# RWKV-7 recurrence on one core: from 64-row and 64-column products per head to products on the whole TensorE array

## The chip, the cores and the metric

One core of a Trainium2 chip runs the whole program. The metric is the device time of one execution in microseconds (us), the median of several executions. Five engines work side by side, each through its own instructions in order: PE (TensorE, matrix products), DVE (VectorE), ACT (ScalarE), POOL (GpSimd) and SP, which here issues the DMAs.

## The reference, cut to what matters

The program is one step of a hybrid layer: 512 prompt frames and 32 sample frames, a combined input projection, three recurrences (Mamba-2 SSD, GLA, RWKV-7), output projections and a cross attention. The change touches the RWKV-7 branch, 16 heads of 64 x 64 state:

```python
def step(S, inp):
    r_t, w_t, k_t, v_t, kk_t, a_t = inp
    s_kk = jnp.einsum('bhvk,bhk->bhv', S, kk_t)
    S_new = (S * w_t[:, :, None, :] - s_kk[..., None] * (kk_t * a_t)[:, :, None, :]
             + v_t[..., None] * k_t[:, :, None, :]).astype(S.dtype)
    return S_new, jnp.einsum('bhvk,bhk->bhv', S_new, r_t)
...
o7, rwkv_new = _rwkv7_scan(r_h, hd(decay), k_h, v_h, kk, a_h, rwkv_h)
```

## The kernel before

**Tiling.** The frames are cut into chunks of 64: eight of the prompt (c = 0 to 7) and one of the sample (c = 8). Two heads share the 128 partitions (partitions 0 to 63 and 64 to 127), so there are eight pairs p of heads. Within a chunk the recurrence is written as matrix products with an inverse of a 64 x 64 triangular matrix; from chunk to chunk a state Sn is handed on. All products of the recurrence are plain float32; the profile records each of them as two MATMUL rows. The dense projections (tile pd, weights wh and wl, activations uh and ul) are split into high and low float32r parts, one row per product, 48 products for each of 158 blocks of 128 output columns.

**Threads per pair.** rw_A(p) (line 815) prepares the operands: AR (decayed keys in AR[.., 0, :], decayed queries in AR[.., 1, :]), PP (products of keys, tile pp), TK (values and keys by token, through DRAM). rw_I(p) (line 984) inverts: a DMA brings blocks of PP to tile nd, 31 pairs of POOL operations (im, td; lines 1011 and 1012) do the substitution, the result goes through DRAM into TT, is transposed on DVE (line 1022), and two sets of 32-row products (pW, pT) finish it. rw_C(p) (line 1043) is the recurrence, nine steps, c = 8 first. rw_N(p) normalises. The tiles AR, PP, TT, TK, GC of a pair stand in one of three slots.

**One step of rw_C** (lines 1063 to 1102) comes to PE three times, with other engines between:

- first visit (lines 1072 to 1077): keys times state, per head, to pa, and state times queries, per head, to po: four products of 64 x 64. DVE then forms R (line 1079).
- second visit (line 1083): the inverse TT times R, per head: two products of 64 x 64. ACT copies head 0 into TK and DVE head 1 (lines 1084, 1085).
- third visit (lines 1089 and 1092): the state update pS and the output po, per head, 128 rows by 64 columns: four products. DVE makes the new state Sn (line 1097), ACT copies the output into AR (line 1102).

At c = 0 there is no state yet, and the first visit is left out. So there are 64 first, 72 second and 72 third visits.

**Order.** A planner, class Sched (line 126), runs at build time. Every thread is a generator; the planner keeps estimated times for each engine, takes the ready thread of the highest priority and writes its instructions out. The dense products fill the time in which no thread of higher priority is ready, at most five between two looks (GRAIN = 5). mm() (line 226) holds the estimate of a product, with 90 and 105 ns for a change between float32r and float32. The result is a fixed order per engine; nothing is rearranged when it runs. The last 48 dense blocks of the projection (gates) have no one waiting for them until the end and serve as fill for the RWKV part and then for the GLA and SSD part.

Of the kernel before, what the change touches and what calls it, by code (L numbers as in the profile page):

```python
# [8 lines left out]
F32 = mybir.dt.float32  # L9
F32R = mybir.dt.float32r  # L10
I32 = mybir.dt.int32
# [114 lines left out]
class Sched:  # L126
# [99 lines left out]
    def mm(self, out, lhsT, rhs, start, stop, transpose=False, shared=False):  # L226

        n = rhs.free_size()
        k, m = lhsT.partition_size(), lhsT.free_size()
        if transpose:  # L230
            self.nc.tensor.transpose(out, lhsT, rhs)
            ns = 107.0
        else:
            self.nc.tensor.matmul(out, lhsT, rhs, start=start, stop=stop, skip_group_check=shared)  # L234
            if lhsT.dtype == F32R:
                ns = n / 2.4 + 12.7
            elif m <= 64:
                ns = max(60.0, n * 0.95 + 14)
            else:
                ns = max(210.0, n * 1.67)  # L240
        small = lhsT.dtype != F32R
        if self.small and not small:
            ns += 105
        elif small and not self.small:
            ns += 90
        self.small = small
        self.n_small = self.n_small + ns if small else 0.0
        if start:
            self.note("pe", ns, (out,), (lhsT, rhs))
        else:  # L250
            self.note("pe", ns, (), (lhsT, rhs))
            self.mark(out, 0, "pe", self.t["pe"])
# [72 lines left out]
def body(tc, I, O):  # L325
    nc = tc.nc
# [4 lines left out]
    def has(*names):  # L331
        return lambda: all(n in done for n in names)
# [12 lines left out]
    with tc.manual_schedule(), \  # L345
# [370 lines left out]
        EE = rwp.tile([128, 9, 65], F32, name="EE")  # L716

        def make_slot(pool, i):
            d = dict(AR=pool.tile([128, 9, 2, 64], F32, name=f"AR{i}"))
            d["PP"] = pool.tile([128, 9, 2, 2, 64], F32, name=f"PP{i}")  # L720
            d["TT"] = pool.tile([128, 9, 64], F32, name=f"TT{i}")
            d["TK"] = pool.tile([128, 2, 9, 2, 64], F32, name=f"TK{i}")
            d["GC"] = pool.tile([128, 9, 1], F32, name=f"GC{i}")
            return d
# [76 lines left out]
        def rows64(scr, h):  # L801

            return scr[:, h, 0:4096].rearrange("c (s t) -> s c t", t=64)
# [5 lines left out]
        def ch(a):  # L809
            return a.rearrange("p (c t) -> p c t", t=64)  # L810
# [4 lines left out]
        def rw_A(p):  # L815
# [3 lines left out]
            if p == 2:  # L819
                yield has("rwR")  # L820
            d = slot[p % NSLOT]
            w2h = rwp.tile([128, 2, 128], F32R, name="w2h", tag="w2h")
            yield S.stored(w2r)
            yield S.at(w2r)
# [68 lines left out]
            S.tt(ch(k7), ch(ks), tha, MUL, e="p")  # L893
            if p >= NSLOT:
                yield has(f"rwO{p - NSLOT}")
            ar = d["AR"]
            S.tt(ar[:, :, 0, :], ch(kk), EE[:, :, 0:64], MUL)
            yield S.free("v")
            S.stt(be, ch(kka), -0.5, Gi, MUL, MUL)
            S.cp(bk[64:128, :, 2, :], be[64:128])  # L900
            yield has(f"rs{p}")
            yield S.at(rs)
            S.tt(ar[:, :, 1, :], ch(rs), EE[:, :, 1:65], MUL)
            yield S.free("v")
            bee = sq
            gcol = d["GC"]
# [35 lines left out]
            for c0, cn in ((0, 4), (4, 4), (8, 1)):  # L942
                ps = []
                for _ in range(2):
                    ps.append((yield from bank("pp")))
                for c in range(cn):
                    for i in range(2):
                        hs = slice(64 * i, 64 * i + 64)
                        S.mm(ps[i][:, c * 128:c * 128 + 128], bk[hs, c0 + c, i:i + 2, :].rearrange("p a t -> p (a t)"),
                             ar[hs, c0 + c].rearrange("p a t -> p (a t)"), True, True)  # L950
                for i in range(2):
                    S.tt(pp[:, c0:c0 + cn, i].rearrange("p c a t -> p c (a t)"), ps[i][:, :cn * 128].rearrange("p (c x) -> p c x", c=cn),
                         C("m_rw").unsqueeze(1).to_broadcast([128, cn, 128]), MUL)
                yield S.free("v")
# [29 lines left out]
        def rw_I(p):  # L984
# [31 lines left out]
                S.store(out=blocks(d_scr)[:, g:32:3], in_=td[g * NB:g * NB + NB, 0:m])  # L1016
            yield S.stored(td)
            for h in range(2):
                S.dma(out=tt_[h * 64:h * 64 + 64], in_=rows64(d_scr, h))
            yield S.at(tt_)  # L1020
            x1 = rwr.tile([128, 8, 32], F32, name="x1", tag="itmp")
            nc.vector.transpose(x1, tt_[:, 0:8, 0:32])
            S.note("v", 340, (x1,), (tt_,))
            yield S.at(x1) + W["XM"]
            ps = yield from bank("pW")
            for c in range(8):
# [5 lines left out]
            ps = yield from bank("pT")  # L1032
            for c in range(8):
                for h in (0, 64):
                    S.mm(ps[h:h + 32, c * 32:c * 32 + 32], w[h + 32:h + 64, c, :], tt_[h + 32:h + 64, c, 32:64], True, True)
            for h in (0, 64):
                S.act(tt_[h:h + 32, 0:8, 32:64], ps[h:h + 32, :256].rearrange("p (c t) -> p c t", t=32), AF.Copy)
            done.add(f"rwI{p}")
            yield None

        IE = "pv"[W["IE"]]

        def rw_C(p):
# [12 lines left out]
            for c0, cn in ((4, 5), (0, 4)):  # L1056
                ps = yield from bank("pr")
                for c in range(cn):
                    for i in range(2):
                        hs, gs = slice(64 * i, 64 * i + 64), slice(64 - 64 * i, 128 - 64 * i)  # L1060
                        S.mm(ps[hs, c * 64:c * 64 + 64], PP[gs, c0 + c, i, 0, :], VU[gs, c0 + c, i, :], True, True)
                S.act(RV[:, c0:c0 + cn].rearrange("p c t -> p (c t)"), ps[:, :cn * 64], AF.Copy)
            for c in [8] + list(range(8)):
                Ss = s0r if c == 8 else (None if c == 0 else st_)
                pa = yield from bank("pc")
                pb = yield from bank("pc")
                pu = pa[:, 64:128], pb[:, 0:64]
                po, pS = pb[:, 64:128], pa[:, 128:192]
                if Ss is None:
                    R = RV[:, 0]  # L1070
                else:
                    for h in (0, 64):
                        hs = slice(h, h + 64)
                        S.mm(pa[hs, 0:64], AR[hs, c, 0, :], Ss[hs, :], True, True)
                    for h in (0, 64):
                        hs = slice(h, h + 64)
                        S.mm(po[hs], Ss[hs, :], AR[hs, c, 1, :], True, False, shared=True)
                    R = rwp.tile([128, 64], F32, name="R", tag="R", bufs=2)
                    S.tt(R, pa[:, 0:64], RV[:, c], ADD)
                yield S.at(R)  # L1080
                for i, h in enumerate((0, 64)):
                    hs = slice(h, h + 64)
                    S.mm(pu[i][hs], TTt[hs, c, :], R[hs, :], i == 0 or Ss is None, True, shared=i == 1)
                S.act(VU[0:64, c, 0, :], pu[0][0:64], AF.Copy)
                S.cp(VU[64:128, c, 1, :], pu[1][64:128])
                yield S.at(VU[0:64, c, 0, :], VU[64:128, c, 1, :]) + W["R2"]
                for i in range(2):
                    hs = slice(64 * i, 64 * i + 64)
                    S.mm(pS[hs], KB[:, c, i, :], VU[:, c, i, :], True, True)
                for i in range(2):  # L1090
                    hs = slice(64 * i, 64 * i + 64)
                    S.mm(po[hs], VU[:, c, i, :], PP[:, c, i, 1, :], Ss is None, True, shared=True)
                ns = rwp.tile([128, 64], F32, name="Sn", tag="S", bufs=2)
                if Ss is None:
                    S.cp(ns, pS)
                else:
                    S.stt(ns, Ss, GC[:, c, :], pS, MUL, ADD)
                if c >= 7:
                    S.store(out=O["rwkv_s" if c == 8 else "rwkv_p"][:, p], in_=ns)
                st_ = ns  # L1100
                yield S.at(ns)
                S.act(AR[:, c, 1, :], po, AF.Copy)
            done.add(f"rwC{p}")

        def rw_N(p):
# [2 lines left out]
            rwr = pools["rwR"][1]  # L1108
            d = slot[p % NSLOT]
            AR = d["AR"]  # L1110
            o7 = AR[:, :, 1, :]
            HC = ((0, 4, 0), (4, 4, 256), (8, 1, 512))

            def rows(t, c, n, o):
# [903 lines left out]
```

## Time and profile before

| what | us |
|---|---|
| median of three runs | 1344.29 (1342.06 to 1345.19) |
| the profiled execution | 1338.43 |
| its span, first to last instruction | 1336.6 |
| PE busy in the span | 1292.2 (97%) |
| DVE, ACT, POOL busy | 790.7, 633.8, 348.6 |

The span has four parts on PE: memory projections and the start (to about 190 us), the RWKV recurrence (194.5 to 630.5), GLA and SSD (about 710 to 932), and then gates, output projections and attention. Of a group of matrix products the busy time tells little, since records overlap: a record lasts some 290 ns while the next begins 125 ns later. What a product takes from PE is read as the distance from its start to the start of the next one.

### The profile page before, as it was taken

How to read it: one execution, taken by the hardware profiler on the slowest of the kernel's cores; microseconds unless marked ns; L12 is line 12 of the kernel's file. 1: busy time of each engine (PE TensorE's matmuls, PEld its weight loads, DVE VectorE, ACT ScalarE, POOL GpSimd, SP SyncE). 2: the span in 40 equal slices, each digit the busy share in tenths (PEclk: the TensorE clock that was granted, in tenths of full speed). 3: DMA queues.
4: the chain of work that ended last, by engine and by line, in shares of the span. 5: the costliest groups of instructions: out<-in, count | busy, mean ns of one | idle time of the engine just before them, and what ended most of it. 6: DMA issues, size and time to landing. Idle time of an engine off the chain costs nothing.

```text
span 1336.6 us, 28525 instructions
## 1 busy us (share of the span) xinstructions
PE 1292.2 (97%) x11416; PEld 1209.0 (90%) x11416; DVE 790.7 (59%) x1578; ACT 633.8 (47%) x1221; POOL 348.6 (26%) x712
## 2 busy tenths in 40 slices
PE   7899999999999999999899999999999999999997
PEld 6799998888888888898899989898999999989996
DVE  5747765756646574333546887863466756575543
ACT  4665455465655553353636355362545323544421
POOL 2701827356362724520112532420000000000000
PEclk9999999999999999999999999999999999999998
DMA  8443554445444354432421423432697446530301
GB/s 289 152 141 100 153 136 110 105 119 127 126 105 117 108 149 115 137 130 84 156 99 63 148 88 115 140 113 75 230 328 245 145 131 201 175 118 25 102 17 67
DMA packets 167557, 176.67 MB, mean 132 GB/s; under 512 B 99825, under 2 KB 122449, under 8 KB 167297
## 3 DMA queue, kind: packets, MB, share of 16 engines
q1 hardware_dynamic: 167280, 174.71, 42.9%
q8 instruction: 90, 1.47, 0.5%
q14 instruction: 43, 0.34, 0.1%
q10 hardware_dynamic: 144, 0.14, 0.0%
HBM read 134.01 MB, written 33.16 MB: 125 GB/s over the span
## 4 chain that ended last, share of the span: by engine, by line
PE 63%; DVE 4%; ACT 2%; DMA 2%; issue 1%; SPq 0%; DVEq 0%; ACTq 0%
PE pd L234 50%; PE pc L234 3%; PE py L234 1%; PE psc L234 1%; PE pO L234 1%; PE pov L234 1%; DMA wraw<-in_wall 1%; PE ph L234 1%; PE pp L234 1%; PE pss L234 1%; PE pS L234 1%; DVE wr L273 1%; DMA ab<-acs_d 1%; ACT L267 0%; PE pr L234 0%
## 5 line engine op out<-in xcount | busy, mean ns | idle before, releaser
L234 PE MATMUL pd<-uh,wl 128*128 128x272 f32 (+1 forms) x1632 | 483.9, 297 | 9.2 <-DVE wl L273 5.0
L234 PE MATMUL pd<-uh,wh 128*128 128x272 f32 (+1 forms) x1632 | 484.3, 297 | 0.0
L234 PE MATMUL pd<-ul,wh 128*128 128x272 f32 (+1 forms) x1632 | 476.6, 292 | 0.0
L234 PEld LDWEIGHTS pd<-uh,wl 128*128 128x128 f32 (+1 forms) x1632 | 307.4, 188 | 18.4 <-DVE wl L273 10.3
L234 PEld LDWEIGHTS pd<-uh,wh 128*128 128x128 f32 (+1 forms) x1632 | 307.7, 189 | 8.2 <-issue 2.4
L234 PEld LDWEIGHTS pd<-ul,wh 128*128 128x128 f32 (+1 forms) x1632 | 307.7, 189 | 4.2 <-issue 1.2
L273 DVE TENSOR_TENSOR wl<-wraw,wh 128x1024 fp32r<-128x1024 f32 x142 | 180.1, 1268 | 62.8 <-ACT wh L267 61.9
L267 ACT ACTIVATE wh<-wraw 128x1024 fp32r<-128x1024 f32 x142 | 149.6, 1054 | 66.0 <-PE pd L234 47.0
L234 PE MATMUL pd<-uh,wr 128*128 128x256 f32 (+1 forms) x768 | 152.6, 295 | 2.7 <-ACT uh L267 2.7
L234 PEld LDWEIGHTS pd<-uh,wr 128*128 128x128 f32 x768 | 122.4, 190 | 5.5 <-ACT uh L267 3.1
L273 POOL TENSOR_TENSOR macc<-macc,hrs 128x288 f32<-128x288 f32 x3 | 3.0, 1022 | 426.4 <-ACT hrs L267 426.4
L273 POOL TENSOR_TENSOR im<-td,nd 108x84 f32<-108x84 f32 (+23 forms) x248 | 89.1, 359 | 91.0 <-DMA nd<-n_scr 60.5
L234 PE MATMUL pd<-ul,wr 128*128 128x256 f32 (+1 forms) x384 | 111.3, 290 | 0.1
L273 POOL TENSOR_TENSOR td<-td,im 108x84 f32<-108x84 f32 (+23 forms) x248 | 99.2, 400 | 19.4
L234 PEld LDWEIGHTS pd<-ul,wr 128*128 128x128 f32 x384 | 73.0, 190 | 0.7 <-DVE ul L273 0.4
L267 ACT ACT_TABLE_LOAD x55 | 70.6, 1283 | 3.3 <-DVE tB L273 2.3
L278 DVE SCALAR_TENSOR_TENSOR fg<-fg,pd 128x272 f32<-128x272 f32 x48 | 20.6, 432 | 53.6 <-ACT fg L267 53.3
L267 ACT ACTIVATE TK<-pc 64x64 f32<-64x64 f32 x72 | 15.3, 213 | 72.0 <-PE pc L234 71.9
L267 ACT ACTIVATE lerpA<-pd,par 128x272 f32<-128x272 f32 x50 | 24.2, 485 | 44.2 <-PE pd L234 40.0
L234 PE MATMUL pd<-mnh,wh 128*128 128x256 f32 x128 | 37.0, 289 | 7.9 <-ACT mnh L267 6.7
L284 POOL TENSOR_SCALAR cs<-cs,par 128x544 f32<-128x544 f32 x8 | 8.3, 1043 | 139.3 <-DVE cs L273 51.5
L267 ACT ACTIVATE fg<-pd,dpar 128x272 f32<-128x272 f32 x48 | 23.2, 484 | 38.6 <-PE pd L234 30.8
(480 smaller groups left out, 2480.9 us busy)
## 6 DMA issues: line engine op xcount, KB each, us to landing
wraw<-in_wall SPq DMA_DIRECT2D x166, 512.0 KB
g_mg<-fg SPq DMA_DIRECT2D x24, 272.0 KB
mgt<-g_mg SPq DMA_DIRECT2D x24, 272.0 KB
TK<-tm SPq DMA_DIRECT2D x96, 64.0 KB
ab<-acs_d SPq DMA_DIRECT2D x8, 512.0 KB
nd<-n_scr SPq DMA_DIRECT2D x24, 144.0 KB
n_scr<-PP SPq DMA_DIRECT2D x16, 144.0 KB
TT<-d_scr SPq DMA_DIRECT2D x16, 144.0 KB
```

The costliest lines, as they stand in the source:

```text
L234: self.nc.tensor.matmul(out, lhsT, rhs, start=start, stop=stop, skip_group_check=shared)
L267: self.nc.scalar.activation(out=out, in_=in_, func=f, scale=scale, bias=bias)
L273: eng.tensor_tensor(out=out, in0=a, in1=b, op=op)
L278: self.nc.vector.scalar_tensor_tensor(out=out, in0=a, scalar=s, in1=b, op0=op0, op1=op1)
L284: eng.tensor_scalar(out=out, in0=a, scalar1=s1, scalar2=s2, op0=op0, **kw)
```

## The change

Both heads of a pair are now computed by one product on all 128 rows and columns, with the operands laid out as block diagonals:

- AR gets three parts: the keys of head 0 (zero in partitions 64 to 127), the keys of head 1 (zero in 0 to 63), the queries. TT becomes 128 wide, with the two inverses on its diagonal and zeros elsewhere. The zeros are written once per slot by four POOL memsets.
- First visit: one product (AR's two key parts, 128 x 128, with the state, 64 columns). The product of state and queries moves to the third visit.
- A new POOL operation per step forms Sd, the state as a block diagonal (128 x 128, state times a mask of ones).
- Second visit: one product of TT with R repeated twice (128 columns). One DVE copy_predicated with the mask takes both diagonal blocks into TK, in place of one copy on ACT and one on DVE.
- Third visit: three products of 128 x 128 with 128 columns: pS (both heads' keys with TK), po from Sd and the queries, po from TK and PP. Of pS and po only the diagonal blocks are used: DVE makes Sn, and ACT copies the output, in two halves of 64 partitions each.
- The transposes of TT on DVE are two of 64 partitions in place of one of 128.
- In the planner's estimate a "small" product is now one with under 128 rows or columns, whatever its type, and the change back costs 150.

```diff
-        small = lhsT.dtype != F32R
+        small = k < 128 or m < 128
         if self.small and not small:
-            ns += 105
+            ns += 150
...
-            d = dict(AR=pool.tile([128, 9, 2, 64], F32, name=f"AR{i}"))
+            d = dict(AR=pool.tile([128, 9, 3, 64], F32, name=f"AR{i}"))
-            d["TT"] = pool.tile([128, 9, 64], F32, name=f"TT{i}")
+            d["TT"] = pool.tile([128, 9, 128], F32, name=f"TT{i}")
...
+            if p < NSLOT:
+                for h in (0, 64):
+                    g = 64 - h
+                    for x in (d["AR"][h:h + 64, :, g // 64, :], d["TT"][h:h + 64, :, g:g + 64]):
+                        nc.gpsimd.memset(x, 0.0)
+                        S.note("p", 700, (x,), ())
...
-            S.tt(ar[:, :, 0, :], ch(kk), EE[:, :, 0:64], MUL)
-            yield S.free("v")
+            for i in range(2):
+                hs = slice(64 * i, 64 * i + 64)
+                S.tt(ar[hs, :, i, :], ch(kk)[hs], EE[hs, :, 0:64], MUL)
+                yield S.free("v")
...
-                S.dma(out=tt_[h * 64:h * 64 + 64], in_=rows64(d_scr, h))
+                S.dma(out=tt_[h * 64:h * 64 + 64, :, h * 64:h * 64 + 64], in_=rows64(d_scr, h))
...
-                    for h in (0, 64):
-                        hs = slice(h, h + 64)
-                        S.mm(pa[hs, 0:64], AR[hs, c, 0, :], Ss[hs, :], True, True)
-                    for h in (0, 64):
-                        hs = slice(h, h + 64)
-                        S.mm(po[hs], Ss[hs, :], AR[hs, c, 1, :], True, False, shared=True)
+                    S.mm(pa[:, 0:64], AR[:, c, 0:2, :].rearrange("p a t -> p (a t)"), Ss, True, True)
                     R = rwp.tile([128, 64], F32, name="R", tag="R", bufs=2)
                     S.tt(R, pa[:, 0:64], RV[:, c], ADD)
+                    Sd = rwp.tile([128, 2, 64], F32, name="Sd", tag="Sd", bufs=2)
+                    S.tt(Sd, both(Ss), two(C("blk1")), MUL, e="p")
                 yield S.at(R)
-                for i, h in enumerate((0, 64)):
-                    hs = slice(h, h + 64)
-                    S.mm(pu[i][hs], TTt[hs, c, :], R[hs, :], i == 0 or Ss is None, True, shared=i == 1)
-                S.act(VU[0:64, c, 0, :], pu[0][0:64], AF.Copy)
-                S.cp(VU[64:128, c, 1, :], pu[1][64:128])
-                yield S.at(VU[0:64, c, 0, :], VU[64:128, c, 1, :]) + W["R2"]
+                S.mm(pu, TTt[:, c, :], both(R), True, True)
+                nc.vector.copy_predicated(VU[:, c], two(C("blk1").bitcast(I32)), two(pu))
+                S.note("v", 203, (VU[:, c],), (pu,))
+                yield max(S.at(VU[:, c]), 0.0 if Ss is None else S.at(Sd))
+                S.mm(pS, KB[:, c].rearrange("p a t -> p (a t)"), VU[:, c], True, True)
+                if Ss is not None:
+                    S.mm(po, Sd.rearrange("p a t -> p (a t)"), both(AR[:, c, 2, :]), True, False)
+                S.mm(po, VU[:, c].rearrange("p a t -> p (a t)"), PP[:, c, :, 1, :], Ss is None, True)
+                ns = rwp.tile([128, 64], F32, name="Sn", tag="S", bufs=2)
                 for i in range(2):
                     hs = slice(64 * i, 64 * i + 64)
-                    S.mm(pS[hs], KB[:, c, i, :], VU[:, c, i, :], True, True)
-                for i in range(2):
-                    hs = slice(64 * i, 64 * i + 64)
-                    S.mm(po[hs], VU[:, c, i, :], PP[:, c, i, 1, :], Ss is None, True, shared=True)
...
+                    if Ss is None:
+                        S.cp(ns[hs], pS[hs, hs])
+                    else:
+                        S.stt(ns[hs], Ss[hs], GC[hs, c, :], pS[hs, hs], MUL, ADD)
...
-                S.act(AR[:, c, 1, :], po, AF.Copy)
+                for i in range(2):
+                    hs = slice(64 * i, 64 * i + 64)
+                    S.act(AR[hs, c, 2, :], po[hs, hs], AF.Copy)
```

What this makes of the order on each engine is seen in two places. The first is one step of the recurrence of the second pair (p = 1) on PE, before. In a row stand the tile written, the tiles read, and the rows and columns of the moving operand; "x2" is two in a row; numbers after a name tell tiles apart.

```order
L234 MATMUL pc<-Sn,AR_123 64x64 x2
L234 MATMUL pc<-AR_123,Sn 64x64 x2
L234 MATMUL pd<-uh,wh 128x272
...
L234 MATMUL pc<-R,TT_125 64x64 x2
L234 MATMUL pd<-uh,wl 128x272
...
L234 MATMUL pc<-TK_126 64x64 x2
L234 MATMUL pc<-PP_124,TK_126 64x64 x2
L234 MATMUL pn<-k_3509,blk_96 128x288 x4
```

The same pair's step in the changed kernel, on PE:

```order
L234 MATMUL pd<-uh,wl 128x272
L234 MATMUL pc<-Sn,AR_123 128x64
L234 MATMUL pp<-AR_118,bk 128x128 x2
...
L234 MATMUL pc<-R,TT_125 128x128
L234 MATMUL pd<-uh,wl 128x272
...
L234 MATMUL pc<-TK_126 128x128
L234 MATMUL pc<-AR_123,Sd 128x128
L234 MATMUL pc<-PP_124,TK_126 128x128
L234 MATMUL pbn<-r_3477,blk_96 128x272 x2
```

Ten products of half height or half width have become five of full height and width, and the product with the queries has moved behind the second visit, with Sd as its other operand.

The second place is POOL between the inverses of the pairs p = 1 and p = 2 (im and td are the substitution, bk and ks belong to the preparation of a later pair), before:

```order
L273 TENSOR_TENSOR im<-td,nd 108x11
L273 TENSOR_TENSOR td<-td,im 108x11
L284 TENSOR_SCALAR bk<-bk,dpar 128x9x64
L273 TENSOR_TENSOR ks_109<-ks_109,bk 128x576
L273 TENSOR_TENSOR im<-td,nd 108x31
L273 TENSOR_TENSOR td<-td,im 108x31
```

The same place on POOL in the changed kernel:

```order
L273 TENSOR_TENSOR im<-td,nd 108x11
L273 TENSOR_TENSOR td<-td,im 108x11
L284 TENSOR_SCALAR bk<-bk,dpar 128x9x64
L273 TENSOR_TENSOR ks_109<-ks_109,bk 128x576
L273 TENSOR_TENSOR Sd<-Sn,con 128x128 x3
L273 TENSOR_TENSOR Sd<-s0r,con 128x128
L273 TENSOR_TENSOR im<-td,nd 108x31
L273 TENSOR_TENSOR td<-td,im 108x31
```

The new operations stand in POOL's one queue, behind the preparation's and between the substitution's; 64 of them in all.

Counted over the whole order of PE: stretches of products with under 128 rows or columns that stand between products of full size are 277 before and 96 in the changed kernel; dense products between the first and the last product of the recurrence are 2026 before and 2203 in the changed kernel, and between the first and the last product of GLA and SSD 1205 and 1166.

## Rows read from the trace of the kernel before

**Rows 1.** From the page: busy time, its share of the span and the instructions of each engine; then PE's busy tenths in 40 equal slices of the span.

```profile
PE 1292.2 (97%) x11416; PEld 1209.0 (90%) x11416; DVE 790.7 (59%) x1578; ACT 633.8 (47%) x1221; POOL 348.6 (26%) x712
...
PE   7899999999999999999899999999999999999997
```

**Rows 2.** Who PE waited for over the span, as total us, times, longest us: the first and the last of 17 rows, longest in total first. The 17 totals sum to 35.0.

```profile
PE pd L234 <- DVE wl L273: 7.3, 9, 4.1
...
PE pc L234 <- DVE R L273: 0.3, 1, 0.3
```

**Rows 3.** PE in order of time in one step of the recurrence: start us, length, what, rows * columns of the array and the moving operand's shape, number of records.

```profile
400.35 0.29 PE L234 MATMUL pd<-uh,wl 128*128 128x272 f32 x1
400.57 0.33 PE L234 MATMUL pc<-Sn,AR 64*64 64x64 f32 x4
400.73 0.28 PE L234 MATMUL pc<-AR,Sn 64*64 64x64 f32 x4
400.95 0.39 PE L234 MATMUL pd<-uh,wh 128*128 128x272 f32 x1
401.18 0.29 PE L234 MATMUL pd<-ul,wh 128*128 128x272 f32 x1
401.30 0.29 PE L234 MATMUL pd<-uh,wl 128*128 128x272 f32 x1
...
402.18 0.30 PE L234 MATMUL pd<-uh,wh 128*128 128x272 f32 x1
402.41 0.33 PE L234 MATMUL pc<-R,TT 64*64 64x64 f32 x4
402.67 0.39 PE L234 MATMUL pd<-ul,wh 128*128 128x272 f32 x1
402.90 0.29 PE L234 MATMUL pd<-uh,wl 128*128 128x272 f32 x1
403.02 0.29 PE L234 MATMUL pd<-uh,wh 128*128 128x272 f32 x1
403.15 0.29 PE L234 MATMUL pd<-ul,wh 128*128 128x272 f32 x1
403.27 0.29 PE L234 MATMUL pd<-uh,wl 128*128 128x272 f32 x1
...
403.87 0.39 PE L234 MATMUL pd<-uh,wh 128*128 128x272 f32 x1
```

**Rows 4.** PE in order of time in the GLA part: float32 products of full height and width (pS, pO) among dense ones.

```profile
715.39 0.29 PE L234 MATMUL pd<-ul,wh 128*128 128x272 f32 x1
715.51 0.60 PE L234 MATMUL pS<-vt,kt 128*128 128x256 f32 x2
715.95 0.38 PE L234 MATMUL pO<-AT,vt 128*128 128x128 f32 x2
...
716.62 0.39 PE L234 MATMUL pO<-g_qe,gS 128*128 128x128 f32 x2
...
716.97 0.29 PE L234 MATMUL pd<-uh,wh 128*128 128x272 f32 x1
```

**Rows 5.** PE in order of time in the attention: two float32 products of full height and width with only 32 columns (pts, four records) among float32r ones.

```profile
1261.02 0.53 PE L234 MATMUL pov<-pts,vs 128*128 128x32 f32 x4
1261.38 0.48 PE L234 MATMUL pov<-pT,vh 128*128 128x256 f32 x2
1261.70 0.28 PE L234 MATMUL pov<-pT,vl 128*128 128x256 f32 x1
```

**Rows 6.** Three stretches of the span (from:to in us, length): busy time and instructions of PE, PEld, DVE, ACT and POOL, then PE's granted clock, DMA share and GB/s. The first is the recurrence, the last GLA and SSD, the second stands between them.

```profile
194.50:630.50 436.00, 433.21 (x4568) 381.36 (x4567) 231.14 (x547) 219.63 (x489) 194.65 (x483) 0.99 0.44 119
664.20:667.60 3.40, 2.91 (x13) 2.91 (x14) 3.31 (x5) 0.78 (x2) 0.00 (x0) 0.50 0.53 114
710.00:932.00 222.00, 217.50 (x1830) 203.76 (x1828) 158.48 (x310) 109.36 (x199) 67.85 (x86) 0.99 0.34 108
```

**Rows 7.** The substitution's products on POOL: number, shortest, median and longest ns, first and last start; and what POOL waited for before them (us in total, times).

```profile
L273 POOL TENSOR_TENSOR im<-td,nd x248: 210/320/1357, 133.9 to 575.3; 108x84 f32<-108x84 f32 x12, 108x54 f32<-108x54 f32 x8, 108x90 f32<-108x90 f32 x8, 108x72 f32<-108x72 f32 x8
...
  DMA nd<-n_scr: 60.5, 5
```

**Rows 8.** All engines in order of time, in the step of rows 3: a DVE row and a POOL row.

```profile
400.16 1.37 DVE L876 TENSOR_TENSOR_SCAN EE<-con,EE 128x585 f32<-128x585 f32 x1
...
400.33 1.27 POOL L273 TENSOR_TENSOR td<-td,im 108x45 f32<-108x45 f32 x1
```

**Rows 9.** Groups of POOL by line and shape: busy us, mean ns of one, idle before.

```profile
L273 POOL TENSOR_TENSOR cs<-cs,bo 128x544 f32<-128x544 f32 x8 | 12.6, 1572 | 0.7
...
L273 POOL TENSOR_TENSOR TK<-mem 128x256 f32<-128x256 f32 x8 | 6.7, 868 | 4.0 <-DMA mem<-in_memT 4.0
```

**Rows 10.** Groups of DVE by line and shape: the new state of a step, and the two copies with a mask that this kernel has, in GLA.

```profile
L278 DVE SCALAR_TENSOR_TENSOR Sn<-Sn,GC,pc 128x64 f32<-128x64 f32 x56 | 15.6, 279 | 36.1 <-PE pc L234 33.2 <-ACT AR L267 1.3 <-ACT tm L267 0.9
...
L1255 DVE COPY_PREDICATED AT<-m_ssd,pA 64x512 f32<-64x512 int32 x4 | 2.9, 722 | 0.7 <-PE pA L234 0.7
...
L1256 DVE COPY_PREDICATED AT<-m_ssd,pA 64x256 f32<-64x256 int32 x4 | 1.8, 450 | 0.1
```

**Rows 11.** PE in order of time near the end of the recurrence: the first visits of two steps that follow each other.

```profile
616.24 0.33 PE L234 MATMUL pc<-Sn,AR 64*64 64x64 f32 x4
...
619.60 0.33 PE L234 MATMUL pc<-Sn,AR 64*64 64x64 f32 x4
```

More of the change, by code (lines that the diff above doesn't have):

```diff
@@ L246, in mm @@
         self.small = small
-        self.n_small = self.n_small + ns if small else 0.0
+        self.n_small = self.n_small + ns if lhsT.dtype != F32R else 0.0
         if start:
@@ L902, in rw_A @@
             yield S.at(rs)
-            S.tt(ar[:, :, 1, :], ch(rs), EE[:, :, 1:65], MUL)
+            S.tt(ar[:, :, 2, :], ch(rs), EE[:, :, 1:65], MUL)
             yield S.free("v")
@@ L949, in rw_A @@
                         S.mm(ps[i][:, c * 128:c * 128 + 128], bk[hs, c0 + c, i:i + 2, :].rearrange("p a t -> p (a t)"),
-                             ar[hs, c0 + c].rearrange("p a t -> p (a t)"), True, True)
+                             ar[hs, c0 + c, i:3:2 - i], True, True)
                 for i in range(2):
@@ L1018, in rw_I @@
             for h in range(2):
-                S.dma(out=tt_[h * 64:h * 64 + 64], in_=rows64(d_scr, h))
+                S.dma(out=tt_[h * 64:h * 64 + 64, :, h * 64:h * 64 + 64], in_=rows64(d_scr, h))
             yield S.at(tt_)
             x1 = rwr.tile([128, 8, 32], F32, name="x1", tag="itmp")
-            nc.vector.transpose(x1, tt_[:, 0:8, 0:32])
-            S.note("v", 340, (x1,), (tt_,))
+            for h in (0, 64):
+                nc.vector.transpose(x1[h:h + 64], tt_[h:h + 64, 0:8, h:h + 32])
+                S.note("v", 340, (x1[h:h + 64],), (tt_[h:h + 64],))
             yield S.at(x1) + W["XM"]
@@ L1034, in rw_I @@
                 for h in (0, 64):
-                    S.mm(ps[h:h + 32, c * 32:c * 32 + 32], w[h + 32:h + 64, c, :], tt_[h + 32:h + 64, c, 32:64], True, True)
+                    S.mm(ps[h:h + 32, c * 32:c * 32 + 32], w[h + 32:h + 64, c, :], tt_[h + 32:h + 64, c, h + 32:h + 64], True, True)
             for h in (0, 64):
-                S.act(tt_[h:h + 32, 0:8, 32:64], ps[h:h + 32, :256].rearrange("p (c t) -> p c t", t=32), AF.Copy)
+                S.act(tt_[h:h + 32, 0:8, h + 32:h + 64], ps[h:h + 32, :256].rearrange("p (c t) -> p c t", t=32), AF.Copy)
             done.add(f"rwI{p}")
@@ L1041, in body, with two, both @@
         IE = "pv"[W["IE"]]
+        def two(a):
+            return a.rearrange("p (a t) -> p a t", a=2)
+        def both(a):
+            return a.unsqueeze(1).to_broadcast([128, 2, 64])
         def rw_C(p):
@@ L1066, in rw_C @@
                 pb = yield from bank("pc")
-                pu = pa[:, 64:128], pb[:, 0:64]
-                po, pS = pb[:, 64:128], pa[:, 128:192]
+                pu, pS, po = pa[:, 128:256], pa[:, 256:384], pb[:, 0:128]
                 if Ss is None:
@@ L1093, in rw_C @@
[L1093 to L1097, printed above, removed]
+                    if Ss is None:
+                        S.cp(ns[hs], pS[hs, hs])
+                    else:
+                        S.stt(ns[hs], Ss[hs], GC[hs, c, :], pS[hs, hs], MUL, ADD)
                 if c >= 7:
@@ L1110, in rw_N @@
             AR = d["AR"]
-            o7 = AR[:, :, 1, :]
+            o7 = AR[:, :, 2, :]
             HC = ((0, 4, 0), (4, 4, 256), (8, 1, 512))
```

## The prediction

> **What bounds the kernel now.** I read the page first: PE is busy for 97% of the span, and of 40 slices only four stand below 9 tenths: the first two, one in the middle and the last [rows 1]. Then who PE waits for: 17 kinds of waits sum to 35.0 us, most of it in the start and at the seams between the parts; the recurrence's own tiles R and Sn end next to none of it [rows 2]. So the sum of what PE is given to do sets the time, and the question for each stretch is what a product takes from PE, not how long it lasts. That is read from starts.
>
> In one step of the recurrence dense products follow each other every 0.125 us (403.02, 403.15, 403.27). From the dense product before the first visit (400.35) to the third one behind it (401.30) there are 0.95 us, of which 3 x 0.125 is dense work: the visit takes **0.575 us** for four products. The second visit, by the same reading (402.18 to 403.02), takes 0.84 - 0.375 = **0.465 us** for only two. The third, with four products again, spans the same 0.60 us from the dense product before it to the one behind it as the first (403.27 to 403.87, 400.35 to 400.95), so 0.575 too [rows 3]. Two equations: four products and a visit 0.575, two and a visit 0.465, so a small product takes **0.055 us** and the coming and going **0.355 us** a visit. It shows in the rows: 0.22 instead of 0.125 from the last dense product to the first small one, 0.23 from the first dense product behind to the next.
>
> Do float32 products of full height and width pay this too? In GLA they stand among the same dense ones: 0.12 us from the dense product to the first of them, so nothing on entry; three pO products of 128 columns take 716.62 - 715.95 = 0.67 us, **0.223 us** each; and from the last one to the second dense product behind are 0.35 us, which is one product and one dense product, so nothing on leaving [rows 4]. With few columns they cost as much: two of 32 columns take 0.36 us to the next product, and the next pair takes 0.32 where two of 256 columns would need about 0.24, so 0.44 in all, 0.22 each [rows 5]. The visit's price is for the small tile, not for float32.
>
> The Trainium skill says the same from both ends. TensorEngine Tiling (Array Packing), section Key Properties, says that a change of tiling mode drains the array; the 0.355 us above agree. Its section Overview recommends tiles for small operands, since several run at once, and that speaks against this change: by it alone five full products in place of ten packed ones only lose.
>
> **The change, part by part.**
>
> *Products.* There are 64 first, 72 second and 72 third visits, 64 x 10 + 8 x 6 = 688 small products, at 0.055 that is 37.8 us. In their place stand 64 x 5 + 8 x 3 = 344 full ones; at 0.222 they take 76.4 us. Alone that is 38.6 us more.
>
> *Visits.* Some visits shared their coming and going with other small products (pr, pp, or two visits in a row), and pr, pp, pW, pT keep theirs. The count over the whole order of PE takes that in: 277 stretches of small products become 96, so 181 x 0.355 = 64.3 us less. In sum 64.3 + 37.8 - 76.4 = **25.7 us less work for PE**. If a full product cost 0.21 or 0.24 the gain would be 30 or 20.
>
> *Does the time follow?* Only where PE has other work in its place. The recurrence is not paced by PE: two steps can follow each other in 3.36 us [rows 11], 72 of them would need 242 us, and it lasts 436 [rows 6]. It is paced by the inverses, whose first and last substitution start 133.9 and 575.3 us into the span [rows 7]. Dense products fill the rest, and the new order moves 2203 - 2026 = 177 of them, 22 us, into this stretch. So the stretch hardly gets shorter and the later ones get less to do. Of the moved products 1205 - 1166 = 39 are missing in GLA and SSD, where PE already has 222.0 - 217.5 = 4.5 us without work [rows 6]. I take that part as lost: 39 x 0.125 = **4.9 us**; the bounds are 0 and 25.7 (all moved work missed somewhere).
>
> *POOL.* 64 operations Sd of 128 elements. POOL took 868 ns for 256 and 1572 for 544 elements of two tiles [rows 9]; along that line 128 take 0.56 us, 36 us in all, beside 194.7 us that POOL is busy in the 436 [rows 6]. The substitution stands in the same queue, so a pair's inverse can get later by up to 9 x 0.56 = 5 us; dense work covers that as long as fill is left. The new wait is PE's third visit for Sd. What is queued behind it on PE is everything. Sd can start with the new state, before the first visit (400.57), and is needed 2.7 to 2.9 us later (the third visit stands between 403.27 and 403.87) [rows 3]. That is five times its length. Late it comes where POOL's queue is held: by the first im of an inverse, which waits for its DMA (60.5 us in 5 waits [rows 7]), or by a long DVE operation: td took 1.27 us beside a scan of 1.37 us, the median im takes 0.32 [rows 7, 8]. Most of the 60.5 us POOL would have stood idle anyway. I take four places of 1 us, **4 us**; the bounds are 0 and the slower rival below.
>
> *DVE and ACT.* The two copies with a mask put 128 columns at about 0.31 us (450 for 256, 722 for 512), a new state in two halves at twice 0.28 at most [rows 10]. DVE gets some 0.3 us per step, 22 us in a stretch where it is busy 231 of 436 us [rows 6]; the chain of a step grows by about as much, and it does not set the pace. ACT trades one copy for another. Cover gone, that would be 72 x 0.3 = 22 us.
>
> *Once only.* Twelve memsets for three slots, eight more transposes and split products, the same number of DMAs: beside dense work, nothing.
>
> *Clock.* PE ran at half clock, 1.2 GHz, for 3.4 us after its longest wait, at 664.2 [rows 6]. One such stretch more or less is 1.7 us; I take no change, and 5 us either way.
>
> Sum: 25.7 - 4.9 - 4 = 16.8, rounded to **17 us**. The profiled execution took 1338.43 us, so 1321; the median of the runs is 5.9 us above it, and 1344.29 - 17 gives **1327 us**.
>
> **The rivals.**
>
> A, the forecast: PE's work goes down by 20 to 30 us, and 0 to 15 are lost again. 1313 to 1337.
>
> B, given back: the stretch of the recurrence stays as long as the inverses make it, POOL makes these longer, fill is used up there, and GLA and SSD or the seams stand idle for all that was saved. Nothing is left: 1338 to 1347. For it speaks that fill moves forward; against it that only 39 of the 177 moved products are missing in GLA and SSD, the others in the last part, where nothing but PE's sum counts.
>
> C, slower: Sd is late in most steps, and PE, with all dense work behind it, stands each time. It decides from 25.7 / 64 = 0.4 us a step on. If every Sd came 0.8 us late, 51 us would be lost: 1344 - 26 + 51 = 1369. For it: one queue with the substitution, with longest operations of 1.36 us [rows 7]. Against it: 2.7 us of room, and the median.
>
> The Trainium skill, SBUF - State Buffer, section SBUF: two separate sides, has the rule behind this rival: VectorE and GpSimd share a pair of ports, and an operation that holds it blocks the other engine's for its whole length. The td beside the scan agrees.
>
> D, the change doesn't do what it says: the visit's price is paid by the full float32 products too, and only the packing is lost. Then 38.6 us more: 1383. Rows 4 speak clearly against it, but they are of another part.
>
> **How the numbers follow.** A 0.70, B 0.17, C 0.10, D 0.03. A run of this kernel can be told from no change from about 0.2% on, 2.7 us. Faster by more: A and half of B, with a little for doubt, 0.80. Within: 0.08. Slower: C, D and the late end of B, 0.12. The range leaves out C and D above (0.13) and some 0.05 below: from 1313 (30 us saved, little lost) to 1345 (all given back).
>
> **What would show it.** In the changed profile: the third visit entered 0.125 us after a dense product, not 0.22; full pc products 0.22 us apart; 181 visits less; POOL some 36 us busier; PE's waits with perhaps 5 to 10 us more in sum, for Sd by name and in GLA and SSD. Wrong I would be if waits for Sd summed to more than 25 us, if full products cost over 0.30 us each (344 x 0.08 would eat the gain), or if the dense products behind a visit still stood 0.23 us apart.

## The result, and the profile after

| | before | after |
|---|---|---|
| median of six runs each, us | 1341.90 (1340.32 to 1345.19) | 1348.48 (1345.96 to 1351.26) |
| the profiled execution, its span | 1338.43, 1336.6 | 1347.95, 1346.2 |
| mean granted clock of PE over the span | 0.990 | 0.982 |

The change makes the kernel 0.6% slower: ratio 1.0057, 95% interval 1.0038 to 1.0076. Forecast were 17 us less; it is 6.6 more.

The page of after, against [rows 1]: busy time and instructions, PE's busy tenths, and the granted clock in tenths.

```profile
PE 1284.0 (95%) x10728; PEld 1235.6 (92%) x10728; DVE 833.0 (62%) x1666; ACT 638.3 (47%) x1221; POOL 407.7 (30%) x788
...
PE   7899998999999999999989999998999999999997
...
PEclk9999999999989999999989998999999999999998
```

PE has less to do, but three inner slices now stand at 8, before one, and three inner ones show a lower clock, before none. POOL is 59 us busier, DVE 42. Whom PE waited for, against [rows 2] (total us, times, longest us; all totals sum to 52.5, before 35.0):

```profile
PE pd L234 <- DVE wl L273: 11.1, 9, 2.6
...
PE pc L234 <- POOL Sd L273: 5.5, 5, 1.7
PE pc L234 <- DVE TK L1098: 5.0, 6, 2.5
PE pc L234 <- DVE R L273: 4.1, 5, 3.0
...
PE pdt L231 <- DVE smt L278: 2.8, 1, 2.8
```

The recurrence's own products (pc) waited 1.1 us before and 14.6 now. One third visit and the next first visit of after, on PE in order of time, against [rows 3]:

```profile
401.71 0.29 PE L234 MATMUL pd<-ul,wh 128*128 128x272 f32 x1
401.83 0.38 PE L234 MATMUL pc<-TK 128*128 128x128 f32 x2
402.05 0.39 PE L234 MATMUL pc<-AR,Sd 128*128 128x128 f32 x2
402.27 0.39 PE L234 MATMUL pc<-PP,TK 128*128 128x128 f32 x2
402.42 0.38 PE L234 MATMUL pw<-lww,w2h 128*128 128x288 f32 x1
402.63 0.29 PE L234 MATMUL pw<-lww,w2l 128*128 128x288 f32 x1
...
403.27 0.33 PE L234 MATMUL pc<-Sn,AR 128*128 128x64 f32 x2
403.41 0.37 PE L234 MATMUL pd<-uh,wh 128*128 128x272 f32 x1
403.62 0.29 PE L234 MATMUL pd<-ul,wh 128*128 128x272 f32 x1
```

The visit is entered 0.12 us after a dense product, the full products start 0.22 apart, and leaving takes 0.36 for one full and one other product: no price of the visit, as forecast. So the work went down and the standing went up. The clock, by stretches of after (from:to and length; busy time of PE, PEld, DVE, ACT, POOL; granted clock, DMA share, GB/s):

```profile
376.80:379.50 2.70, 0.04 (x1) 0.00 (x0) 2.67 (x2) 0.00 (x0) 2.62 (x3) 1.00 0.86 238
379.50:386.30 6.80, 6.48 (x35) 5.92 (x36) 3.58 (x10) 1.37 (x4) 5.53 (x18) 0.50 0.37 81
513.00:515.40 2.40, 0.00 (x0) 0.00 (x0) 2.37 (x4) 0.00 (x0) 2.24 (x4) 1.00 0.00 0
516.00:519.40 3.40, 3.40 (x18) 3.40 (x16) 3.29 (x6) 1.08 (x4) 3.14 (x6) 0.50 0.79 241
```

PE stands for 3.0 and 2.5 us, and then runs at 1.2 GHz for 6.8 and 3.4 us. DVE is busy throughout, with what stands ahead of R and TK in its queue; POOL is busy beside it.

**An account.** The span is PE's own work at full clock, its waits, and span x (1 - mean clock) for the lower clock. Before: 1336.6 - 35.0 - 13.4 = **1288.2** of work. After: 1346.2 - 52.5 - 24.2 = **1269.5**. So 18.7 us less work, 17.5 more waits, 10.8 more lost to the clock. The clock's part is that of one execution: over the 26 runs of before beside e13 it goes from 12.0 to 20.1 us, over six of after from 18.8 to 27.0, so a few us in it say little.

### The profile page after: what moved, and what is told of

Read it like the earlier page. It is cut to its first block, busy times and chain, and to the rows that moved or that the text cites. A ratio compares the mean times of both kernels' runs of the same rounds, so it can differ in the third digit from the quotient of the medians.

```text
span 1346.2 us, 27384 instructions
## 1 busy us (share of the span) xinstructions
PE 1284.0 (95%) x10728; PEld 1235.6 (92%) x10728; DVE 833.0 (62%) x1666; ACT 638.3 (47%) x1221; POOL 407.7 (30%) x788
## 5 line engine op out<-in xcount | busy, mean ns | idle before, releaser
L234 PEld LDWEIGHTS pd<-uh,wl 128*128 128x128 f32 (+1 forms) x1632 | 311.0, 191 | 19.1 <-DVE wl L273 14.9
L234 PEld LDWEIGHTS pd<-uh,wh 128*128 128x128 f32 (+1 forms) x1632 | 311.5, 191 | 4.3 <-issue 2.6
L234 PEld LDWEIGHTS pd<-ul,wh 128*128 128x128 f32 (+1 forms) x1632 | 311.3, 191 | 1.9 <-issue 1.1
L273 POOL TENSOR_TENSOR im<-td,nd 108x84 f32<-108x84 f32 (+23 forms) x248 | 100.4, 405 | 65.7 <-DMA nd<-n_scr 22.5
L273 POOL TENSOR_TENSOR Sd<-Sn,con 128x128 f32<-128x128 f32 x56 | 33.7, 601 | 69.9 <-DVE Sn L278 46.2
L290 POOL COPY convo<-xp 128x3 f32<-128x3 f32 x24 | 9.7, 437 | 148.7 <-ACT xp L267 148.7
L267 ACT ACTIVATE AR<-pc 64x64 f32<-64x64 f32 x144 | 30.9, 214 | 40.9 <-PE pc L234 40.0
```

Source lines behind the costliest of these rows:

```text
L267: self.nc.scalar.activation(out=out, in_=in_, func=f, scale=scale, bias=bias)
L273: eng.tensor_tensor(out=out, in0=a, in1=b, op=op)
L290: (self.nc.vector if e == "v" else self.nc.gpsimd).tensor_copy(out=out, in_=a)
```

## The experiments

Theory 1: Sd on POOL is the loss, by PE's wait for it (1a) or by holding up DVE and the inverses (1b). Theory 2: PE comes back as early as DVE can at best be ready, and every late DVE operation stops it. Theory 3: work brought forward is missed later. Theory 4, formed after the first four runs: the operations are worth what was forecast, and the planner happened to give them an order with bad places. "Before" is run beside each kernel; ratios are to it.

| kernel | median us | ratio, 95% interval | waits of PE (of pc) | clock loss | PE's work |
|---|---|---|---|---|---|
| after | 1348.5 | 1.0057 (1.0038 to 1.0076) | 52.5 (14.6) | 24.2 | 1269.5 |
| e1, no Sd | 1323.3 | 0.9862 (0.9845 to 0.9878) | 39.0 (4.2) | 15.9 | 1268.2 |
| e2, Sd on ACT | 1325.7 | 0.9890 (0.9876 to 0.9905) | 41.2 (5.1) | 10.6 | 1271.0 |
| e3, before, other estimate | 1332.4 | 0.9936 (0.9921 to 0.9951) | 32.5 (2.7) | 8.0 | 1289.6 |
| e4, after, old estimate | 1354.9 | 1.0096 (1.0079 to 1.0113) | 55.7 (21.0) | 21.6 | 1273.5 |
| e5, POOL in e2's order | 1341.8 | 1.0008 (0.9997 to 1.0018) | 51.3 (15.5) | 16.1 | 1272.3 |
| e6, e2 with unread POOL operation | 1328.3 | 0.9910 (0.9895 to 0.9926) | 41.0 (5.4) | 11.9 | 1272.2 |
| e7, ACT in after's order | 1346.2 | 1.0040 (1.0024 to 1.0056) | 53.6 (14.2) | 24.2 | 1268.2 |
| e8, before with unread POOL operation | 1341.7 | 1.0004 (0.9990 to 1.0018) | 33.7 (1.1) | 14.7 | 1287.8 |
| e9, after, another order | 1326.7 | 0.9903 (0.9884 to 0.9922) | 42.0 (11.6) | 11.9 | 1269.2 |
| e10, e2, another order | 1330.8 | 0.9932 (0.9915 to 0.9950) | 42.2 (6.5) | 15.9 | 1271.0 |
| e11, before, another order | 1344.1 | 1.0026 (1.0012 to 1.0041) | 40.7 (3.9) | 14.8 | 1292.3 |
| e12, after, another order | 1330.6 | 0.9937 (0.9918 to 0.9956) | 42.0 (9.5) | 14.6 | 1270.7 |
| e13, after, two places | 1341.7 | 1.0015 (1.0004 to 1.0026) | 49.1 (10.7) | 18.7 | 1270.9 |
| e14, before, e12's edit | 1338.4 | 0.9991 (0.9977 to 1.0004) | 33.1 (3.4) | 10.7 | 1289.6 |
| e15, e2, e12's edit | 1329.6 | 0.9924 (0.9909 to 0.9940) | 42.6 (10.8) | 10.6 | 1273.2 |
| e16, after, another order | 1344.3 | 1.0037 (1.0022 to 1.0053) | 52.3 (10.7) | 24.2 | 1267.1 |
| e17, after, three places | 1345.6 | 1.0034 (1.0017 to 1.0051) | 50.5 (11.9) | 22.9 | 1271.1 |

The last column is worked out as above. It is 1267 to 1274 in all fourteen kernels with the changed products (mean 1270.6) and 1288 to 1292 in the five with the old ones, before among them (mean 1289.5): **18.9 us less work, whatever the order**.

**Is it Sd?**

```diff
- S.tt(Sd, both(Ss), two(C("blk1")), MUL, e="p")
+ Sd = two(C("blk1"))                          # e1
...
+ Sd = sds[c % 2]                              # e2: zeros written once
+ for i in range(2):
+     S.act(Sd[hs, i, :], Ss[hs], AF.Copy)     # hs: 64 partitions
```

e1: 

> The changed kernel without the POOL operation Sd: the second product of the third visit reads a fixed mask tile instead of the state, so the output of the recurrence lacks the state's part; every product and every other operation stays. Theory 1 (the new POOL operation is the loss: 64 of 601 ns make POOL's and, through what they hold up, DVE's part of a step late): the PE waits for Sd (5.5 us) go, and those for R and TK (4.1 and 5.0) fall to the 1 us in sum that the kernel before had; with some 8 us of half clock that follow such stops, 1320 to 1329. Theory 2 (the order leaves PE no room: it comes back for R and TK at the earliest time, and any late DVE operation stops it): only Sd's own 5.5 us go, R and TK stay above 6 us in sum: 1339 to 1344. Theory 3 (work brought forward is missed later): 1345 to 1350.

e2: 

> The changed kernel with Sd made by two ACT copies of its diagonal blocks into two tiles whose zeros are written once, in place of the POOL multiplication. Theory 1 (POOL's operation): as without Sd, 1320 to 1331, PE's waits for Sd under 1 us, R and TK about 1 us. Theory 2 (no room in the order): waits for Sd under 2 us, R and TK above 6 us in sum, 1339 to 1345. If ACT cannot do 128 short copies beside its other work, waits on ACT appear and the time stays at 1348.

Both times came out as Theory 1 has it, against Theories 2 and 3, and e2 beats both kernels. The waits fell less than Theory 1 has it: R and TK 3.3 us in e1 and 2.9 in e2, Sd 1.3 in e2. And each edit also changed what the planner reckons with, and so the order of everything.

**The estimates.** e3 raises the 90 and 105 ns of the kernel before to 140 and 155; e4 puts the three old lines of mm() back into after.

e3: 

> The kernel before, with nothing but the planner's estimate of coming to and leaving float32 products raised by 50 ns each, so that its visits are planned at about what they measure (195 + 100, against some 0.3 to 0.355 us). No operation is added or taken away; only the order follows the new estimate. Theory 2 (in the kernel before PE ran behind the plan by what its visits cost more than estimated, and this lag hid late DVE and POOL operations): the recurrence now shows waits of PE for R, TK and Sn of 8 us or more in sum, before 1 us, and the time is 1350 to 1367. Theory 1: no such waits, 1337 to 1346.

e4: 

> The changed kernel with the old rule of the estimate put back: each full float32 product of a visit is again planned with 90 and 105 ns for coming and going, which rows of the changed kernel do not show. Theory 2: PE is really ahead of the plan by up to 0.2 us a visit, the others are late against it, and the waits for Sd, R and TK grow from 14.6 to over 22 us: 1356 to 1375. Theory 1: the order is nearly the same for POOL and DVE, 1344 to 1352.

e3 contradicts both theories: 8 us faster, from a new order alone. e4 is slower, near the range of Theory 2 but not by its way: the waits for Sd grew to 11.3 us, while those for R and TK fell from 9.1 to 5.9, 17.2 in sum where over 22 were expected.

**Operation or order.** e5 and e7 swap the operation and keep the order; e6 and e8 add the POOL operation with nobody reading it.

```diff
  # e5: order of e2, where the planner reckons with ACT
- S.act(Sd[hs, i, :], Ss[hs], AF.Copy)
+ nc.gpsimd.tensor_tensor(out=Sd, in0=both(Ss), in1=two(C("blk1")), op=MUL)
  # e7: order of after, where it reckons with POOL
- S.tt(Sd, both(Ss), two(C("blk1")), MUL, e="p")
+ nc.scalar.activation(out=Sd[hs, i, :], in_=Ss[hs], func=AF.Copy)
  # e6 on e2, e8 on before
+ nc.gpsimd.tensor_tensor(out=Sx, in0=both(Ss), in1=two(C("blk1")), op=MUL)
```

e5: 

> The order of the kernel with Sd on ACT (1325.7 us) kept as it is on PE, DVE and SP, and only the two ACT copies of each step taken out and the one POOL multiplication put in their place. Theory 1 (the POOL operation itself is the loss, by waits for it or by what it holds up): 1342 to 1352, PE's waits for Sd by name back at 5 us or more. Theory 4 (not the operation but the order that the planner made around it): 1324 to 1331. Without either, half of each: 1333 to 1340.

e6: 

> The kernel with Sd on ACT, its order kept on PE, DVE, ACT and SP, and in every step one POOL multiplication more, of the same operands, into a tile (bfloat16) that nobody reads. No engine waits for its result; what it can do is hold POOL's queue and whatever POOL's work holds up. Theory 1a (the loss is PE's wait for a late Sd): 1325 to 1330. Theory 1b (the loss is what 64 more POOL operations do to DVE and to the inverses): DVE operations beside it get longer, waits for R and TK go from 3 back to 8 us or more, 1336 to 1347.

e7: 

> The changed kernel's order kept on PE, DVE and SP, and only the POOL operation of each step replaced by two ACT copies. Theory 1: the waits for Sd, R and TK (14.6 us) fall to 5 or less, 1323 to 1333. Theory 4 (the order is the loss): it stays at 1342 to 1350.

e8: 

> The kernel before with its order kept, and in each of the 64 steps with a state one POOL multiplication of 128 elements more, into a tile that nobody reads. Theory 1b: DVE and the inverses are held up here too, PE's waits for R, TK and Sn go from 1 to 6 us or more, 1346 to 1358. Theory 1a: nobody waits for it, 1338 to 1344. If the lag of PE behind the plan covers late DVE operations (Theory 2), also 1338 to 1344, with POOL 36 us busier and DVE operations longer.

Theory 1 falls for the changed kernel: e7 has no Sd on POOL and stays at 1346.2, with 8.8 us of waits for R and TK (after 9.1). Its 5.4 us for Sd say less, since this order does not allow for the time of ACT's copies. 1b falls too: 64 unread ones cost 2.5 us in e6 (intervals overlap) and 0.7 in e8 (the interval of its ratio takes in 1). 1a holds in e5, where the order does not allow for POOL's time and the swap costs 16 us against e2; its waits for Sd:

```profile
PE pc L234 <- POOL Sd L1098: 11.2, 9, 2.9
```

In after's order the stops for R and TK came with Sd on ACT too, in e7:

```profile
PE pc L234 <- DVE TK L1104: 5.8, 7, 2.5
PE pc L234 <- ACT Sd L1100: 5.4, 3, 2.3
PE pc L234 <- DVE R L273: 3.0, 3, 2.4
```

**Other orders of the same operations.** One number of the planner is changed, no operation.

```diff
- XM=3000.0                               # allowance behind a transpose of TT
+ XM=2500.0                               # e9 after, e10 e2, e11 before
- def free(self, e, slack=900.0):
+ def free(self, e, slack=700.0):         # e12 after, e14 before, e15 e2
- IS=900.0
+ IS=1100.0                               # e16 after
```

e9: 

> The changed kernel, its operations unchanged, with another order: the planner's allowance behind a transpose of TT is 2500 in place of 3000 ns, a number that has nothing to do with the change. Theory 4 (the changed kernel got an order with bad places; the next order may lack them): anywhere from 1325 to 1342, with the two longest waits of the recurrence (R 3.0, TK 2.5) gone. Theory 1 in its last form (Sd on POOL always costs, as a wait or as a later third visit in the plan): 1342 to 1352, with waits for Sd, R and TK of 10 us or more.

e10: 

> The kernel with Sd on ACT (1325.7 us), with the same number of the planner changed from 3000 to 2500 ns and nothing else. Theory 4 (a scatter of the orders of some 10 us either way): up to 1340 is possible. Theory 1 in its last form: 1320 to 1331.

e11: 

> The kernel before with the same number of the planner changed from 3000 to 2500 ns and nothing else. It says how far a new order alone moves the kernel before. Theory 4: 1330 to 1350, as the order with other estimates gave 1332.4. If orders of this kernel lie close together: 1337 to 1345.

e12: 

> The changed kernel, its operations unchanged, with a planner that lets the other threads queue their DVE and POOL work only up to 700 ns ahead of PE, not 900. Theory 2 (what stands ahead of R and TK in DVE's queue makes them late): the waits for R and TK fall from 9.1 to under 4 us, 1328 to 1340. Theory 1 in its last form: those for Sd stay at 5 us or more, and the time at 1340 to 1350.

e14: 

> The kernel before with the planner number 700 for 900 ns (how far the other threads may queue ahead of PE), the same edit that brought the changed kernel to 1330.6. If that number is worth 18 us to any kernel: 1320 to 1328. If it only gave the changed kernel another order: 1332 to 1346, the range of the three orders of the kernel before.

e15: 

> The kernel with Sd on ACT and the planner number 700 for 900 ns. Orders of this code gave 1325.7 and 1330.8. Theory 4: 1318 to 1333. If both edits mend the same thing: 1326 to 1331; if they add: 1308 to 1318.

e16: 

> The changed kernel, operations unchanged, with one more order: the planner's allowance for POOL's queue in the inverse is 1100 in place of 900 ns. Theory 4: a draw from what orders of these operations give, 1325 to 1350, and the time follows the sum of PE's waits and of the time at half clock, with PE's own work the same as in the other orders to within 3 us.

The changed kernel's own operations, Sd on POOL, take 1326.7, 1330.6, 1344.3, 1348.5 or, with the estimate of e4, 1354.9 us in five orders of the planner; the old ones 1332.4 to 1344.1 in four (e3, with its other estimate, among them); with Sd on ACT 1325.7 to 1330.8 in three, and 1346.2 in after's order (e7). e10, e11 and e15 lie where more than one of their expectations allows; e16 lies in its range, its work 3.5 us off the mean where 3 was expected. e12 went as Theory 2 has it (R and TK fell from 9.1 to 2.8 us of waits, with 4.3 left for Sd); but its edit is worth 1.3 us to the kernel before, within its interval, and makes e2 4 us slower, so it is the order that it gave this kernel. Nor is it the waits of pc alone: e9 has 11.6 us of them and is 22 us faster. It has no stop of 2.8 us at the seam (e12 keeps it, 2.9, and takes 1330.6), and half the clock loss:

```profile
PE pc L234 <- POOL Sd L273: 6.8, 5, 1.8
...
PE pc L234 <- DVE R L273: 3.8, 5, 2.3
```

**Single places.** On DVE of after, in order of time (start us, length), R stands behind long operations of a pair that has time (bk and rn are decayed keys of p = 5):

```profile
375.51 1.21 DVE L273 TENSOR_TENSOR wl<-wraw,wh 128x1024 fp32r<-128x1024 f32 x1
376.65 1.19 DVE L273 TENSOR_TENSOR bk<-ks,bk 128x576 f32<-128x576 f32 x1
377.87 1.77 DVE L273 TENSOR_TENSOR rn<-bk,GC 128x576 f32<-128x576 f32 x1
379.56 0.21 DVE L273 TENSOR_TENSOR R<-pc,RV 128x64 f32<-128x64 f32 x1
```

e13 moves only this and the like place at 513.0; PE, ACT, POOL and SP keep their order.

```diff
  # DVE, first place
- wl, bk, rn, R
+ wl, R, bk, rn
  # DVE, second place
- bk, AR, wl, TK
+ wl, TK, bk, AR
```

e13: 

> The changed kernel with the order kept on PE, ACT, POOL and SP, and on DVE at two places alone: R (the wait of 3.0 us at 376.8) goes ahead of the two long operations bk and rn, and TK (2.5 us at 513.0) ahead of bk and AR. Theory 4, with the bad places as its cause: the two waits shrink to under 1 us each, and the 10.2 us at half clock behind them go, 5 us: 4.5 + 5, so 1336 to 1342. If what PE gains there is lost at its next wait: 1345 to 1350.

6.8 us come back, about the least that Theory 4 expected. DVE of e13 at the first place:

```profile
373.00 1.21 DVE L280 TENSOR_TENSOR wl<-wraw,wh 128x1024 fp32r<-128x1024 f32 x1
374.14 0.21 DVE L280 TENSOR_TENSOR R<-pc,RV 128x64 f32<-128x64 f32 x1
374.27 1.05 DVE L280 TENSOR_TENSOR bk<-ks,bk 128x576 f32<-128x576 f32 x1
375.35 1.77 DVE L280 TENSOR_TENSOR rn<-bk,GC 128x576 f32<-128x576 f32 x1
```

R comes without a stop, and rn is late instead; no wait of PE for it follows, and the 6.8 us at half clock are gone. At the second place 2.5 us became 0.4 for TK and 1.8 one visit on, again with 3.4 us at half clock behind, so nearly all of it went to PE's next wait (the view puts that one down to ACT; the product waits for Sn, which DVE ends at 509.28, just ahead of it):

```profile
PE pc L234 <- ACT wh L267: 1.8, 1, 1.8
PE pc L234 <- DVE TK L1115: 0.4, 1, 0.4
```

The two places together give back 3.3 us of waits and 3.4 of clock, about what was measured. In all, waits fell by 3.4 us and the clock loss by 5.5, a part of it elsewhere.

e17 also moves, on ACT at the seam, wh (5.4 us idle for its DMA) behind the gate operation fg.

e17: 

> The kernel of the two places (1341.7 us), with one more place changed, on ACT alone: at the seam behind the recurrence the conversion of weights wh, which stands 5.4 us for its DMA, goes behind the gate operation fg that stood behind it; the other engines keep their order. PE's waits there were 2.8 us for smt, 1.6 for acsT and 1.3 for wl, with 6.8 us at half clock behind. Theory 4 with single bad places as its cause: the 2.8 go, and half or all of the half clock, 1.7 to 3.4: 1335 to 1338. If PE then waits as long for the weights of the next block: 1340 to 1344.

A miss: 1345.6. With wh out of the way, fg itself stood for a DMA, the store that frees its buffer, and PE still waited 2.5 us for smt, and 2.3 in place of 1.3 for wl. What ACT waited for at the seam of e17:

```profile
ACT fg L267 <- DMA g_ssd<-fg: 6.1, 1, 6.1
```

So in both orders ACT stands at the seam for a transfer; moving one operation did not clear it, and what would is not shown.

## Why the prediction was wrong, step by step

By the account the forecast of 16.8 us less missed by 26.4: work 7.0, waits 8.6, clock 10.8.

*Products and visits: right in kind, a quarter too large.* Forecast 25.7 us, measured 18.9 over all orders. The prices hold: the three visits of a step, between dense products, take 0.227, 0.225 and 0.680 us in the median (from the start of the dense product before to that of the second behind, less two of 0.125), before 0.576, 0.458 and 0.579. A part of the rest is short stops: of 144 such visits of after 25 take over 0.04 us more than the lowest quarter of their kind, without a stop that the waits view shows, 3.9 us in sum (before 1 of 147, 0.2). What the remainder is stays open.

*Sd: right in size, wrong in company.* Forecast 4 us, measured 5.5, while the same stretch brought 4.1 and 5.0 us for R and TK, which stood at nothing. In each of the eight kernels with Sd on POOL PE waits 4.3 to 11.3 us for it, in the four planned with Sd on ACT 0.5 to 1.7 (in e7, where it was not planned, 5.4). So every order tried with Sd on POOL had such waits, of about the forecast size or up to three times that.

*DVE "does not set the pace": the step that failed.* The 22 us more on DVE were put beside dense work, and no wait of PE for R or TK was priced. (Sn and TK got 22.9 us dearer, as forecast; all of DVE 42.) DVE is busy 276.7 us in 194.5:653.4 (before 231.1 in 194.5:630.5 [rows 6]), and what counts is not its sum but what stands ahead of R and TK in its queue. At 376.8 that was three operations of 4.2 us together. The first place of e13 shows that such a place costs PE its wait and the clock behind it.

*The clock: no change forecast, 10.8 us measured*, beyond the 5 us allowed. One stretch of 3.4 us [rows 6] was taken for the size of the thing; but before has five of them ahead of its last 9 us, and after nine, most of them behind a stop of PE. So this term grows with the stops, though not with each (last section). It falls with the first place in e13.

*GLA and SSD: 4.9 us forecast.* Waits from the recurrence's end to 960 us are 15.3, before 9.0: 6.2 more, about as forecast. The agreement is luck: in e9 they are 7.4, with no more dense products in that part (1157, after 1166), so this is the order's too. And 39 leaves out those behind SSD's first product (pcb, at 697.9 us before): from there it is 1248 before, so 82 are missing. The stretch of the recurrence, forecast as hardly shorter, is 22.9 us longer (458.9, before 436.0 [rows 6]).

*The rivals.* C (Sd late in most steps) and D did not happen. B, all given back, came nearest, but not by its way: in e8 64 more POOL operations cost nothing clear of noise. What stood in no rival is that the planner's order is redone by the change and scatters by itself. The forecast time, 1327, is what these operations take in e9; in the order of after they take 22 us more. In the mean, five orders of the change with Sd on POOL stand at 1341.0, four of the old operations at 1339.2, which so few orders of such scatter can't tell apart; with Sd on ACT three orders give 1328.7. Whether Sd on POOL makes bad orders likelier beyond its own waits, or those five were unlucky, stays open. So does what loses the other 15 us of after behind the two places of e13: it is located as waits and clock, not as a cause.

## What to carry to other kernels

Where an order is planned at build time, a change of one operation redraws the whole order: time a change in several orders of either kernel, or hold the order and swap the operation, before the change is credited or blamed. Subtract the waits and the clock loss from the span first; what is left is the work, and here it was within 4 us of its mean in every order. Price a long wait with the clock that may follow it, and look at what stands ahead of the awaited result in its engine's queue, not at that engine's share.

## What the runs showed of the hardware that was not expected

DVE and POOL lengthen each other where both are busy, in either direction. POOL beside the rows of DVE above, in after:

```profile
374.81 2.42 POOL L284 TENSOR_SCALAR cs<-cs,par 128x544 f32<-128x544 f32 x1 [4.28 <-DVE GC L290]
377.31 1.71 POOL L273 TENSOR_TENSOR cs<-cs,bo 128x544 f32<-128x544 f32 x1
378.98 0.96 POOL L273 TENSOR_TENSOR Sd<-s0r,con 128x128 f32<-128x128 f32 x1
```

The first cs takes 2.42 us, in the mean of its group 1.06; rn on DVE beside the second takes 1.77, in the mean 0.95; Sd takes 0.96, in the mean 0.60. The Trainium skill, SBUF - State Buffer, section SBUF: two separate sides, describes an exclusive lock on a pair of ports that the two share, held for a whole instruction, and these rows agree: rn, begun while the second cs runs, ends 0.62 us behind it. Yet e6 and e8 show that 37 and 34 us more of such POOL work, which nobody waits for, moved the time by 2.5 and 0.7 us, neither clear of noise.

PE's stops of 2.5 and 3.0 us in after were followed by 3.4 and 6.8 us at 1.2 GHz, the one of 1.8 us in e13 by 3.4 as well, the one of 1.5 us for Sd at 459.0 in after by none. The length of the stop alone does not tell: three of 1.8 us for Sd in e9 and one of 2.4 us for R in e7 were followed by none, one of 2.1 us at 103 us by 3.4 us in after and by none in before; and 6.8 us at half clock from 826.6 in after follow only stops of 0.4 to 0.8 us and small products. The clock loss of 24.2 us in after is about as large as the whole work that the change was forecast to save.
